# Six modulation rows as one evenly paced stream, from the first mixer to the second feed-forward

## Chip, cores and metric

The kernel runs on one core of a Trainium2 chip. The metric is the device time of one execution in microseconds (us). It is a single program of some 22,000 instructions that runs once per call, and everything in it is float32 (the matmuls use split pairs, below).

## The reference, cut to what matters

Two transformer blocks run one after the other on 256 tokens of width 1024. The first is feed-forward, mixer, feed-forward. The second is modulated by a condition vector `c`, and its context by `c_ctx`:

```python
x = first_block(x, ...)                    # ffn1, mixer1, ffn2
mod  = split(silu(c)     @ w_mod + b_mod, 6)     # six rows of 1024
modc = split(silu(c_ctx) @ w_mod + b_mod, 6)
h  = rmsnorm(x, norm1_g)  * (1 + mod[1])  + mod[0]
hc = rmsnorm(ctx, norm1_g) * (1 + modc[1]) + modc[0]
...                                        # second mixer on h, with states from hc
x  = x + mod[2] * mixer_out
h2 = rmsnorm(x, norm2_g) * (1 + mod[4]) + mod[3]
x  = x + mod[5] * conv_ffn(h2)
```

The change concerns the rows `mod[0..5]` of `c` and `modc[0..1]` of `c_ctx`: vectors that depend on no activations, only on the condition and the weights.

## The kernel before, in words

**Tiling.** Tokens are two blocks of 128 (`TB`). Each weight is streamed from HBM once, in pieces of 128x1024 floats (512 KB, queue of SP, L112, tile `raw`). A piece is split into a rounded high part on ACT (L127, `wh`) and a low part on DVE (L128, `wl`), and each product is three matmuls (`mm3`, L356 to L358). A ring of four split pieces and five raw pieces runs ahead of PE; DVE and ACT are thus needed for every piece that PE uses.

**Stages.** First feed-forward (`f1_gu`, 22 blocks of 48 matmuls, then `f1_dn`, 11 blocks of 24 wider ones), first mixer, its output projection `w_out_t`, second feed-forward (`f2_gu`, `f2_dn`), second mixer, third feed-forward. Behind each down or output projection `residual_norm` (L445) takes the four accumulators through ACT and DVE (sum of squares, gains, residual, norm) and PE transposes the result (L512). While that chain runs, PE has matmuls of the context: `ctx_attn` behind `f1_dn`, `ctx_mlstm` behind `w_out_t`, `ctx_ssd` (pieces `w_ctx` 8 to 10) behind `f2_dn`.

**Side work.** The order of all instructions is fixed when the program is written. `tick` (L197) advances a clock of nominal microseconds at each PE block, and generators registered by `side` (L212) take a step whenever their own time has come. A generator that yields a negative number asks for that much nominal time between steps. `join` (L225) steps a generator until it is done, at one place of the program, whatever its time.

**A modulation row.** `mod_rows` (L940) computes one row as sums of `silu(c)` times rows of `w_mod`, in two halves of 512 columns with eight steps each. A step issues one load of 128x512 floats (256 KB) from the ACT queue (L972), three steps ahead of its use, and one DVE instruction (L978 the first, L980 the others) into an accumulator. Behind eight steps the accumulator is split by ACT (L347) and DVE (L348), one step later PE adds it over the 128 partitions with a pair of matmuls on ones (L957, L958), and one step later DVE adds the bias (L961) and perhaps the gain (L963). Each row ends with three more steps without loads, in which the last sums are finished, and a store of the row by SP (L985). `mod_bcast` (L988) reads rows back where they are used.

**When.** The two rows of `c_ctx` run in the first feed-forward, 3.0 nominal us a step, and `ctx_norm` waits for them. Rows 0 and 1 of `c` start with the first mixer, 6.0 us a step. Rows 2 to 5 start when these and the states of `ctx_mlstm` are done, 2.0 us a step (`more`, L1726). Behind `f2_dn` L1750 joins that generator ahead of `residual_norm`.

Of the kernel before, what the change touches and what calls it, by code (L numbers as in the profile page):

```python
# [9 lines left out]
F32 = mybir.dt.float32  # L10
# [6 lines left out]
D = 1024  # L17
# [9 lines left out]
        ("s_norm_g", 4), ("s_d", 4), ("c", 8), ("c_ctx", 8))  # L27
NCOL = sum(w for _, w in COLS)
NU = 22
NV = 10  # L30
NW = 9
NRAW = 5
RING = 4
# [149 lines left out]
class Net:  # L183
# [753 lines left out]
            yield  # L937


    def mod_rows(self, j, c, gain, out, pace):  # L940


        nc, I = self.nc, self.I
        b = self.u([1, D])
        nc.sync.dma_start(b, I["b_mod_2"][:, j * D:(j + 1) * D])
        if gain is not None:
            g = self.u([1, D])
            nc.sync.dma_start(g, I[gain])
        steps = [(hf, k) for hf in range(2) for k in range(8)]
        ws, ahead, acc = [], 3, None  # L950

        def reduced(acc, hf):
            hi, lo = self.v([128, 512], F32R), self.v([128, 512], F32R)
            self.split(hi, lo, acc)
            yield
            p = self.psA([128, 512])
            nc.tensor.matmul(p[:1], self.onesr[:, :1], hi, start=True, stop=False)  # L957
            nc.tensor.matmul(p[:1], self.onesr[:, :1], lo, start=False, stop=True)  # L958
            yield
            x = self.halves(b)[hf]  # L960
            nc.vector.tensor_tensor(out=x, in0=p[:1], in1=x, op=OP.add)  # L961
            if gain is not None:
                nc.vector.scalar_tensor_tensor(x, x, 1.0, self.halves(g)[hf], op0=OP.add, op1=OP.mult)  # L963

        half = []
        for n in range(len(steps) + ahead + 3):
            for h in half:
                next(h, None)
            if n < len(steps):
                hf, k = steps[n]  # L970
                ws.append(self.v([128, 512]))
                nc.scalar.dma_start(ws[-1], I["w_mod"][j * 8 + k][:, hf * 512:hf * 512 + 512])  # L972
            if 0 <= n - ahead < len(steps):
                hf, k = steps[n - ahead]
                sc = self.silu[c][:, k:k + 1]
                if k == 0:
                    acc = self.v([128, 512])
                    nc.vector.tensor_scalar(acc, ws[n - ahead], sc, None, op0=OP.mult)  # L978
                else:
                    nc.vector.scalar_tensor_tensor(acc, ws[n - ahead], sc, acc, op0=OP.mult, op1=OP.add)  # L980
                if k == 7:
                    half.append(reduced(acc, hf))
            yield -pace
        row = self.dp.tile([1, D], F32, tag=f"mod{c}{j}", name=f"mod_{c}{j}")
        nc.sync.dma_start(row, b)  # L985
        out[c, j] = row

    def mod_bcast(self, c, j):  # L988
        t = self.u([128, D])
# [652 lines left out]
    def program(self, out):  # L1642
# [17 lines left out]
        self.weights.split()  # L1660
        back = self.spill(h, "res0")
        rope = self.side(self.rope_tables(), 40)
        self.mods = {}

        def setup():
            while not hasattr(self, "silu"):
                yield
            for j in range(2):
                yield from self.mod_rows(j, "c_ctx", (None, "norm1_g_2")[j], self.mods, 3.0)

        const = self.side(self.consts(), 4)
        prep = self.side(setup(), 6)
# [32 lines left out]
        self.join(rope, t)  # L1705
        back = self.spill(h, "res1")

        def rows(idx, pace):
            for j in idx:
                yield from self.mod_rows(j, "c", {1: "norm1_g_2", 4: "norm2_g_2"}.get(j), self.mods, pace)  # L1710

        prep = self.side(rows(range(2), 6.0))
        m = [self.u([128, 4, T]) for _ in range(2)]
        mT = self.mixer1(xT, m)
        self.xc = Split(self, 8)
# [7 lines left out]
        self.join(t)  # L1723
        back = self.spill(h, "res2")

        def more():  # L1726
            yield from self.until(states, prep0)
            yield from rows(range(2, 6), 2.0)

        prep0, prep = prep, self.side(more())  # L1730
        hT = self.ffn_up("f2_gu", xT, self.silu_mul)
        self.xc = Split(self, 8)
        cs = self.side(self.ctx_again())
# [1 line left out]
        def gains2(post, gain, shift):  # L1735
            gp["post"] = self.bcast(post) if isinstance(post, str) else self.mod_bcast("c", post)
            gp["pre"], gp["shift"] = self.mod_bcast("c", gain), self.mod_bcast("c", shift)
            gp["h"] = back()
            yield 8
            if isinstance(post, str):  # L1740
                nc.vector.tensor_scalar(gp["post"], gp["post"], 0.5, None, op0=OP.mult)
# [2 lines left out]

        def aside(i):
            if i == 3:
                gs.append(self.side(gains2("ffn2_post_g", 1, 0)))

        acc = self.down("f2_dn", NFF // 2, hT, aside)
        self.join(cs, prep, *gs)  # L1750
        xT, h = Split(self, 8), gp["h"]
        t = self.residual_norm(acc, h, gp["post"], True, gp["pre"], gp["shift"], xT)
        self.ctx_ssd(self.xc)
        self.join(t)
        back = self.spill(h, "res3")

        mT = self.mixer2(xT, lambda: gs.append(self.side(gains2(2, 4, 3))))
        acc = self.down("w_out_2", 4, mT, lambda i: self.weights.presplit(2 * i), 2)
        self.join(*gs)
        xT, h = Split(self, 8), gp["h"]  # L1760
        t = self.residual_norm(acc, h, gp["post"], False, gp["pre"], gp["shift"], xT, ((0, 0, 0, 1, 1, 1, 0, 1, 2, 3),))
        self.join(t)
        back = self.spill(h, "res4")
        hT = self.ffn_up("w_up_t", xT, self.conv_silu_mul)

        def last():
# [155 lines left out]
```

## Time and profile before

| what | value |
|---|---|
| time, median of 3 runs | 1292.15 us (1290.2 to 1292.22) |
| profiled execution: its time, its span | 1290.56 us, 1288.8 us |
| PE busy, DVE busy, ACT busy | 93%, 72%, 48% of the span |
| mean granted clock of TensorE | 0.971 of full speed |
| loads of `w_mod` | 128 of 256 KB, from the ACT queue |
| read from HBM | 241.46 MB, 194 GB/s over the span |

The span runs from the first to the last instruction; the time of an execution is 1.8 us longer here. The page gives busy shares of each engine and the same for 40 slices of the span. A PE that is busy 99% of a slice is the limit there, and whatever other engines do in that slice costs nothing as long as they keep up. A slice in which PE is idle is read from the timeline: the bracket at a row's end is the idle time of that engine just before the instruction and what released it. A clock of 1.00 is the higher of the two levels of TensorE, 2.4 GHz; 0.50 is the lower, 1.2 GHz.

### The profile page before, as it was taken

What the parts mean: (1) busy time and instruction counts of PE and PEld (TensorE: products, weight loads), DVE (VectorE), ACT (ScalarE), POOL (GpSimd) and SP (SyncE); (2) the same over time, 40 slices, a digit from 0 to 9 for tenths busy, and PEclk for the clock granted to TensorE, in tenths of its full rate; (3) what the DMA queues carried; (4) which work ended last, traced back from release to release, by engine and by line L of the source; (5) the groups of instructions that cost most, each with busy time, mean ns of one, the idle gap of its engine ahead of it and who ended that gap; (6) DMA issues with size and microseconds to landing.
All of it is one profiled execution on the core that took longest, in us unless ns stands there. A gap on an engine that the chain in (4) does not pass through costs nothing. (4 is left out here: it accounts for less than half of the span.)

```text
span 1288.8 us, 22199 instructions
## 1 busy us (share of the span) xinstructions
PE 1199.3 (93%) x8728; PEld 1115.0 (87%) x8728; DVE 934.0 (72%) x1603; ACT 624.1 (48%) x1063; POOL 66.9 (5%) x84
## 2 busy tenths in 40 slices
PE   7999998999999999999981699999999998999998
PEld 7999977999878889999860599999888897999977
DVE  4897857667766786767857878589666767888854
ACT  4454545455564464444420454556465344555542
POOL 0020000100000000000000001035100000000000
PEclk8999999999999999999995799999999998999999
DMA  7878785666343766657896355345413265555562
GB/s 265 273 229 256 257 291 195 206 218 218 123 135 116 292 199 221 222 188 247 299 338 216 100 195 190 133 156 172 143 54 100 98 209 216 172 173 181 179 241 85
DMA packets 80605, 251.32 MB, mean 195 GB/s; under 512 B 9523, under 2 KB 10851, under 8 KB 80502
## 3 DMA queue, kind: packets, MB, share of 16 engines
q1 hardware_dynamic: 61654, 215.85, 49.6%
q10 hardware_dynamic: 18432, 33.56, 7.8%
q0 software_dynamic: 416, 0.50, 0.4%
q8 instruction: 68, 1.11, 0.3%
q14 instruction: 35, 0.29, 0.1%
HBM read 241.46 MB, written 8.42 MB: 194 GB/s over the span
## 5 line engine op out<-in xcount | busy, mean ns | idle before, releaser
L128 DVE TENSOR_TENSOR wl<-raw,wh 128x1024 fp32r<-128x1024 f32 (+3 forms) x358 | 424.1, 1218 | 137.0 <-ACT wh L127 133.8
L356 PE MATMUL pB<-u,wh 128*128 128x256 f32 x1696 | 486.6, 287 | 0.7 <-ACT u L347 0.7
L358 PE MATMUL pB<-u,wl 128*128 128x256 f32 x1696 | 481.9, 284 | 1.0 <-DVE wl L128 1.0
L357 PE MATMUL pB<-u,wh 128*128 128x256 f32 x1696 | 481.5, 284 | 0.6 <-DVE u L348 0.3
L127 ACT ACTIVATE wh<-raw 128x1024 fp32r<-128x1024 f32 (+3 forms) x358 | 359.3, 1045 | 93.1 <-PE pB L358 33.8
L356 PEld LDWEIGHTS pB<-u,wh 128*128 128x128 f32 x1696 | 326.0, 192 | 9.4 <-issue 6.8
L358 PEld LDWEIGHTS pB<-u,wl 128*128 128x128 f32 x1696 | 326.0, 192 | 2.3 <-DVE wl L128 1.4
L357 PEld LDWEIGHTS pB<-u,wh 128*128 128x128 f32 x1696 | 326.0, 192 | 1.8 <-DVE u L348 1.4
L356 PE MATMUL pB<-wh,u 128*128 128x512 f32 (+3 forms) x614 | 208.1, 339 | 1.7 <-ACT wh L127 1.7
L357 PE MATMUL pB<-wl,u 128*128 128x512 f32 (+3 forms) x614 | 207.6, 338 | 2.2 <-DVE wl L128 2.0
L358 PE MATMUL pB<-wh,u 128*128 128x512 f32 (+3 forms) x614 | 206.5, 336 | 0.0
L357 PEld LDWEIGHTS pB<-wl,u 128*128 128x128 f32 x614 | 117.0, 191 | 15.7 <-DVE wl L128 5.0
L356 PEld LDWEIGHTS pB<-wh,u 128*128 128x128 f32 x614 | 117.0, 191 | 14.1 <-ACT wh L127 2.4
L358 PEld LDWEIGHTS pB<-wh,u 128*128 128x128 f32 x614 | 117.0, 190 | 11.7
L428 POOL TENSOR_TENSOR rs<-ms,nhalf 128x1 f32<-128x1 f32 (+2 forms) x30 | 28.4, 946 | 877.2 <-DVE ms L422 874.5
L520 ACT ACTIVATE w<-pB 128x256 f32<-128x256 f32 x44 | 16.9, 383 | 116.7 <-PE pB L358 116.3
L980 DVE SCALAR_TENSOR_TENSOR v<-v,silu_c,v 128x512 f32<-128x512 f32 x84 | 62.8, 748 | 12.3 <-DMA v<-w_mod 11.2
L1006 DVE SCALAR_TENSOR_TENSOR w<-pB,cols,w 128x255 f32<-128x255 f32 x120 | 49.6, 476 | 15.8 <-ACT w L1001 10.1
L521 DVE SCALAR_TENSOR_TENSOR w<-w,pB 128x256 f32<-128x256 f32 x44 | 18.5, 420 | 50.2 <-ACT w L520 49.8
L957 PE MATMUL pA<-v,onesr 128*1 128x512 f32 x16 | 7.3, 456 | 42.5 <-ACT v L347 42.5
L356 PE MATMUL pA<-wh,u 128*128 128x256 f32 x132 | 38.5, 292 | 2.4 <-ACT u L347 1.7
L957 PEld LDWEIGHTS pA<-v,onesr 128*1 128x1 f32 x16 | 1.3, 83 | 45.2 <-ACT v L347 45.0
(365 smaller groups left out, 1421.9 us busy)
## 6 DMA issues: line engine op xcount, KB each, us to landing
raw<-f_gu SPq DMA_DIRECT2D x88, 512.0 KB
v<-w_mod ACTq DMA_DIRECT2D x128, 256.0 KB
raw<-w_lat SPq DMA_DIRECT2D x64, 512.0 KB
raw<-f_dn SPq DMA_DIRECT2D x44, 512.0 KB
raw<-w_up_t SPq DMA_DIRECT2D x44, 512.0 KB
raw<-w_ctx SPq DMA_DIRECT2D x22, 512.0 KB
raw<-w_down_t SPq DMA_DIRECT2D x22, 512.0 KB
raw<-w_in_g SPq DMA_DIRECT2D x16, 512.0 KB
```

The source lines that it names most:

```text
L127: nc.scalar.activation(hi, r, AF.Copy)
L128: nc.vector.tensor_tensor(out=lo, in0=r, in1=hi.bitcast(F32), op=OP.subtract)
L356: nc.tensor.matmul(out, a[0], b[0], start=first, stop=False)
L357: nc.tensor.matmul(out, a[0], b[1], start=False, stop=False)
L358: nc.tensor.matmul(out, a[1], b[0], start=False, stop=last)
L428: self.nc.gpsimd.tensor_tensor(out=r, in0=ms, in1=self.nhalf[:, :width], op=OP.pow)
L520: nc.scalar.activation(th, p[:, 0], AF.Tanh, scale=0.5)
L521: nc.vector.scalar_tensor_tensor(th, th, 1.0, p[:, 0], op0=OP.add, op1=OP.mult)
L957: nc.tensor.matmul(p[:1], self.onesr[:, :1], hi, start=True, stop=False)
L980: nc.vector.scalar_tensor_tensor(acc, ws[n - ahead], sc, acc, op0=OP.mult, op1=OP.add)
L1006: nc.vector.scalar_tensor_tensor(y[j][:, o], p[:, j, x], tap(t, i), y[j][:, o], op0=OP.mult, op1=OP.add)
```

## The change

One call of `mod_rows` now takes a list of rows and runs their steps on end: the loads of a row's first steps are issued while the last sums of the row before are finished. The bias and the gain are loaded by halves, into the tiles `v` (12 buffers instead of 10) and no longer into the larger tiles `u`, and each half is added and stored by itself. All six rows of `c` are one generator that starts with the first mixer, 4.2 nominal us a step, and 2.6 from the second feed-forward on; the order of rows is 0, 1, 2, 4, 3, 5. The join of the rows behind `f2_dn` is gone: `need_rows` steps the generator before the place where rows are read back, if they are not done by then, and a join stands behind the second mixer.

```diff
-NV = 10
+NV = 12
...
-    def mod_rows(self, j, c, gain, out, pace):
+    def mod_rows(self, rows, pace):
         nc, I = self.nc, self.I
-        b = self.u([1, D])
-        nc.sync.dma_start(b, I["b_mod_2"][:, j * D:(j + 1) * D])
...
-        steps = [(hf, k) for hf in range(2) for k in range(8)]
+        steps = [(r, hf, k) for r in rows for hf in range(2) for k in range(8)]
...
+            x = self.v([1, 512])
+            nc.sync.dma_start(x, I["b_mod_2"][:, j * D + hf * 512:j * D + hf * 512 + 512])
...
+            nc.sync.dma_start(self.rows[c, j][:, hf * 512:hf * 512 + 512], x)
+            if hf == 1:
+                self.mods[c, j] = self.rows[c, j]
...
-            yield -pace
-        row = self.dp.tile([1, D], F32, tag=f"mod{c}{j}", name=f"mod_{c}{j}")
-        nc.sync.dma_start(row, b)
-        out[c, j] = row
+            yield -pace[0]
+
+    def need_rows(self, side, *keys):
+        while not all(k in self.mods for k in keys):
+            side.step()
...
-            for j in range(2):
-                yield from self.mod_rows(j, "c_ctx", (None, "norm1_g_2")[j], self.mods, 3.0)
+            yield from self.mod_rows([("c_ctx", 0, None), ("c_ctx", 1, "norm1_g_2")], [3.0])
...
-        def rows(idx, pace):
-            for j in idx:
-                yield from self.mod_rows(j, "c", {1: "norm1_g_2", 4: "norm2_g_2"}.get(j), self.mods, pace)
-
-        prep = self.side(rows(range(2), 6.0))
+        pace = [4.2]
+        gain = {1: "norm1_g_2", 4: "norm2_g_2"}
+        rows = self.side(self.mod_rows([("c", j, gain.get(j)) for j in (0, 1, 2, 4, 3, 5)], pace))
...
-        def more():
-            yield from self.until(states, prep0)
-            yield from rows(range(2, 6), 2.0)
-
-        prep0, prep = prep, self.side(more())
+        pace[0] = 2.6
...
             if i == 3:
+                self.need_rows(rows, ("c", 0), ("c", 1))
                 gs.append(self.side(gains2("ffn2_post_g", 1, 0)))
...
-        self.join(cs, prep, *gs)
+        self.join(cs, *gs)
...
-        mT = self.mixer2(xT, lambda: gs.append(self.side(gains2(2, 4, 3))))
+        def aside():
+            self.need_rows(rows, ("c", 2), ("c", 4), ("c", 3))
+            gs.append(self.side(gains2(2, 4, 3)))
+
+        mT = self.mixer2(xT, aside)
...
         back = self.spill(h, "res4")
+        self.join(rows)
```

What this does to the order of instructions is shown at three places. Names ending in `wh` or `wl` are split weights, `pB` the accumulators of a projection, `pA` a smaller one.

PE, between the last matmul of `f2_dn` and the first ones of `w_ctx` 8, before (one more pair stands ahead of these rows, behind that last matmul):

```order
L957 MATMUL pA_7754<-v_7750,onesr 1x512
L958 MATMUL pA_7754<-v_7751,onesr 1x512
L957 MATMUL pA_7803<-v_7795,onesr 1x512
L958 MATMUL pA_7803<-v_7796,onesr 1x512
L957 MATMUL pA_7827<-v_7823,onesr 1x512
L958 MATMUL pA_7827<-v_7824,onesr 1x512
L957 MATMUL pA_7875<-v_7867,onesr 1x512
L958 MATMUL pA_7875<-v_7868,onesr 1x512
L957 MATMUL pA_7898<-v_7894,onesr 1x512
L958 MATMUL pA_7898<-v_7895,onesr 1x512
L356 MATMUL pA_7941<-u_7221,wh_7719 128x256
L357 MATMUL pA_7941<-u_7222,wh_7719 128x256
```

and in the changed kernel at the same place:

```order
L356 MATMUL pB_7440<-wh_7872,u_5676 128x512
L357 MATMUL pB_7440<-wl_7873,u_5676 128x512
L358 MATMUL pB_7440<-wh_7872,u_5677 128x512
L356 MATMUL pB_7440<-wh_7878,u_5676 128x512
L357 MATMUL pB_7440<-wl_7879,u_5676 128x512
L358 MATMUL pB_7440<-wh_7878,u_5677 128x512
L356 MATMUL pA_7971<-u_7433,wh_7922 128x256
L357 MATMUL pA_7971<-u_7434,wh_7922 128x256
L358 MATMUL pA_7971<-u_7433,wl_7923 128x256
```

Six pairs (L957, L958) stood between the last matmul of `f2_dn` and `w_ctx`; none does now. The last pair of the stream stands 48 matmuls earlier, inside `f2_dn`. On DVE the last step of the stream stands in front of the last six splits of weights ahead of the residual chain.

DVE, in the middle of `f2_gu`, before (`w` and `u` are the activation function of a block; L521, L523 and L351 stand once in each block):

```order
L521 SCALAR_TENSOR_TENSOR w_6017<-w_6017,pB_5921 128x256
L523 TENSOR_TENSOR w_6020<-w_6017,pB_5921 128x256
L128 TENSOR_TENSOR wl_6023<-raw_5801,wh_6022 128x1024
L128 TENSOR_TENSOR wl_6029<-raw_5878,wh_6028 128x1024
L351 SCALAR_TENSOR_TENSOR u_5580<-w_6020,u_5579 128x256
L980 SCALAR_TENSOR_TENSOR v_5411<-v_5803,silu_c,v_5411 128x512
```

and in the changed kernel (L984 is L980 of before):

```order
L521 SCALAR_TENSOR_TENSOR w_6137<-w_6137,pB_6038 128x256
L523 TENSOR_TENSOR w_6140<-w_6137,pB_6038 128x256
L128 TENSOR_TENSOR wl_6143<-raw_5899,wh_6142 128x1024
L128 TENSOR_TENSOR wl_6149<-raw_5989,wh_6148 128x1024
L984 SCALAR_TENSOR_TENSOR v_5909<-v_6035,silu_c,v_5909 128x512
L351 SCALAR_TENSOR_TENSOR u_5669<-w_6140,u_5668 128x256
L984 SCALAR_TENSOR_TENSOR v_5909<-v_6080,silu_c,v_5909 128x512
```

A block of `f2_gu` carries two steps instead of one, and so does each block of `f2_dn` up to the tenth.

DVE, in the residual chain behind `w_out_t`, before (the chain of the second token block, then L478, which the first transposes wait for):

```order
L128 TENSOR_TENSOR wl_5273<-raw_5143,wh_5272 128x1024
L438 TENSOR_TENSOR ssq_5283<-ssq_5283,ssq_5280 128x1
L457 TENSOR_TENSOR u_5210<-pB_5039,u_5063 128x512
L457 TENSOR_TENSOR u_5210<-pB_5040,u_5063 128x512
L422 TENSOR_SCALAR ms_988_5289<-ssq_5283 128x1
L460 SCALAR_TENSOR_TENSOR u_5068<-u_5210,rs_989_5291,u_5068 128x512 x2
L478 SCALAR_TENSOR_TENSOR u_5209<-u_5067,rs_973_5235,u_5065 128x512 x2
```

and in the changed kernel:

```order
L128 TENSOR_TENSOR wl_5344<-raw_5213,wh_5343 128x1024
L984 SCALAR_TENSOR_TENSOR v_4931<-v_5155,silu_c,v_4931 128x512
L438 TENSOR_TENSOR ssq_5355<-ssq_5355,ssq_5352 128x1
L457 TENSOR_TENSOR u_5281<-pB_5111,u_5135 128x512
L457 TENSOR_TENSOR u_5281<-pB_5112,u_5135 128x512
L422 TENSOR_SCALAR ms_1013_5361<-ssq_5355 128x1
L460 SCALAR_TENSOR_TENSOR u_5140<-u_5281,rs_1014_5363,u_5140 128x512 x2
L348 TENSOR_TENSOR v_5392<-v_4931,v_5391 128x512
L982 TENSOR_SCALAR v_5401<-v_5194,silu_c 128x512
L478 SCALAR_TENSOR_TENSOR u_5280<-u_5139,rs_998_5306,u_5137 128x512 x2
```

Three instructions of the rows have moved in ahead of L478 there, and one more (L984) stands ahead of the L478 of the second token block. In the first feed-forward the rows of `c_ctx` end some eight weight pieces earlier, and `ctx_norm` with its transposes (L1154) ends inside `f1_dn`; before, its last transposes stood behind it.

## Rows read from the trace of the kernel before

**Rows 1.** Page, parts 1 and 2: PE busy; 40 slices of 32.2 us, in tenths.

```profile
PE 1199.3 (93%) x8728; PEld 1115.0 (87%) x8728; DVE 934.0 (72%) x1603; ACT 624.1 (48%) x1063; POOL 66.9 (5%) x84
...
PE   7999998999999999999981699999999998999998
...
PEclk8999999999999999999995799999999998999999
```

**Rows 2.** Waits of PE, 560 to 800 us: waiter, releaser: us in total, times, longest.

```profile
PE pA L957 <- ACT v L347: 42.5, 5, 9.9
```

**Rows 3.** Timeline of PE around the stall: start us, us, line, operation, [idle before].

```profile
670.94 0.39 PE L358 MATMUL pB<-wh,u 128*128 128x512 f32 x1
...
681.24 0.59 PE L957 MATMUL pA<-v,onesr 128*1 128x512 f32 x1 [9.45 <-ACT v L347]
...
720.61 0.41 PE L356 MATMUL pA<-u,wh 128*128 128x256 f32 x1
...
733.80 1.32 PE L512 MATMUL pB<-ident,u 128*128 128x128 f32 x8 [2.23 <-DVE u L480]
```

**Rows 4.** Windows around it: us; busy PE, PEld, DVE, ACT, POOL; clock; DMA; GB/s.

```profile
675.00:685.00 10.00, 1.18 (x2) 0.16 (x2) 5.62 (x8) 0.63 (x1) 0.00 (x0) 0.50 0.56 180
...
735.00:745.00 10.00, 8.83 (x72) 8.19 (x71) 10.00 (x20) 7.38 (x14) 0.97 (x3) 1.00 0.31 107
```

**Rows 5.** Timelines of DVE and then ACT in the stall.

```profile
692.08 0.69 DVE L348 TENSOR_TENSOR v<-v,v 128x512 fp32r<-128x512 f32 x1 [0.69 <-ACT v L347]
692.69 0.48 DVE L978 TENSOR_SCALAR v<-v,silu_c 128x512 f32<-128x512 f32 x1
...
719.36 0.58 ACT L436 ACTIVATE v<-pB 128x512 f32<-128x512 f32 x1
```

**Rows 6.** Page, a step; windows, steps on DVE; timeline of PE, a covered pair.

```profile
L980 DVE SCALAR_TENSOR_TENSOR v<-v,silu_c,v 128x512 f32<-128x512 f32 x84 | 62.8, 748 | 12.3 <-DMA v<-w_mod 11.2
...
672.00:721.00 49.00, 27.41 (x38) 0.52 0.64 212
...
619.08 0.40 PE L957 MATMUL pA<-v,onesr 128*1 128x512 f32 x1
...
619.55 0.39 PE L356 MATMUL pB<-wh,u 128*128 128x512 f32 x1
```

**Rows 7.** Windows of both feed-forwards: columns as in rows 4.

```profile
40.00:60.00 20.00, 20.00 (x169) 20.00 (x168) 15.49 (x24) 9.28 (x15) 0.00 (x0) 1.00 0.87 298
60.00:80.00 20.00, 20.00 (x167) 19.77 (x167) 19.21 (x40) 9.43 (x15) 4.56 (x8) 1.00 0.80 257
520.00:540.00 20.00, 20.00 (x167) 19.77 (x166) 14.33 (x22) 8.94 (x14) 0.00 (x0) 1.00 0.68 221
620.00:640.00 20.00, 20.00 (x89) 16.32 (x88) 17.40 (x19) 9.97 (x11) 0.00 (x0) 1.00 0.84 294
640.00:660.00 20.00, 19.06 (x83) 15.24 (x82) 9.63 (x11) 5.68 (x6) 0.00 (x0) 1.00 0.92 324
```

**Rows 8.** Timelines of PE and then ACT at the end of the first feed-forward.

```profile
208.94 0.40 PE L358 MATMUL pB<-wh,u 128*128 128x512 f32 x1
209.17 1.04 PE L1154 MATMUL pA<-ident,u 128*128 128x128 f32 x8
211.89 0.38 PE L356 MATMUL pA<-wh,u 128*128 128x256 f32 x1 [1.68 <-ACT u L347]
...
224.80 1.32 PE L512 MATMUL pB<-ident,u 128*128 128x128 f32 x8 [1.51 <-DVE u L478]
...
212.67 0.59 ACT L436 ACTIVATE v<-pB 128x512 f32<-128x512 f32 x1
```

**Rows 9.** Timeline of PE behind the first mixer's output projection; waits in its heads.

```profile
459.72 1.32 PE L512 MATMUL pB<-ident,u 128*128 128x128 f32 x8 [1.13 <-DVE u L478]
...
466.63 1.04 PE L512 MATMUL pB<-ident,u 128*128 128x128 f32 x8
...
PE pB L730 <- DVE v L723: 4.2, 3, 1.5
```

More of the change, by code (lines that the diff above doesn't have):

```diff
@@ L937, in heads_T, with reduced @@
             yield
-    def mod_rows(self, j, c, gain, out, pace):
+    def mod_rows(self, rows, pace):
         nc, I = self.nc, self.I
-        b = self.u([1, D])
-        nc.sync.dma_start(b, I["b_mod_2"][:, j * D:(j + 1) * D])
-        if gain is not None:
-            g = self.u([1, D])
-            nc.sync.dma_start(g, I[gain])
-        steps = [(hf, k) for hf in range(2) for k in range(8)]
+        steps = [(r, hf, k) for r in rows for hf in range(2) for k in range(8)]
         ws, ahead, acc = [], 3, None
-        def reduced(acc, hf):
+        def reduced(acc, c, j, gain, hf):
             hi, lo = self.v([128, 512], F32R), self.v([128, 512], F32R)
             self.split(hi, lo, acc)
+            x = self.v([1, 512])
+            nc.sync.dma_start(x, I["b_mod_2"][:, j * D + hf * 512:j * D + hf * 512 + 512])
+            if gain is not None:
+                g = self.v([1, 512])
+                nc.sync.dma_start(g, I[gain][:, hf * 512:hf * 512 + 512])
             yield
@@ L959, in reduced @@
             yield
-            x = self.halves(b)[hf]
             nc.vector.tensor_tensor(out=x, in0=p[:1], in1=x, op=OP.add)
             if gain is not None:
-                nc.vector.scalar_tensor_tensor(x, x, 1.0, self.halves(g)[hf], op0=OP.add, op1=OP.mult)
+                nc.vector.scalar_tensor_tensor(x, x, 1.0, g, op0=OP.add, op1=OP.mult)
+            if hf == 0:
+                self.rows[c, j] = self.dp.tile([1, D], F32, tag=f"mod{c}{j}", name=f"mod_{c}{j}")
+            nc.sync.dma_start(self.rows[c, j][:, hf * 512:hf * 512 + 512], x)
+            if hf == 1:
+                self.mods[c, j] = self.rows[c, j]
         half = []
@@ L969, in mod_rows @@
             if n < len(steps):
-                hf, k = steps[n]
+                (c, j, gain), hf, k = steps[n]
                 ws.append(self.v([128, 512]))
@@ L973, in mod_rows @@
             if 0 <= n - ahead < len(steps):
-                hf, k = steps[n - ahead]
+                (c, j, gain), hf, k = steps[n - ahead]
                 sc = self.silu[c][:, k:k + 1]
@@ L981, in mod_rows @@
                 if k == 7:
-                    half.append(reduced(acc, hf))
-            yield -pace
-        row = self.dp.tile([1, D], F32, tag=f"mod{c}{j}", name=f"mod_{c}{j}")
-        nc.sync.dma_start(row, b)
-        out[c, j] = row
+                    half.append(reduced(acc, c, j, gain, hf))
+            yield -pace[0]
+    def need_rows(self, side, *keys):
+        while not all(k in self.mods for k in keys):
+            side.step()
     def mod_bcast(self, c, j):
@@ L1662, in program @@
         rope = self.side(self.rope_tables(), 40)
-        self.mods = {}
+        self.mods, self.rows = {}, {}
         def setup():
```

## The prediction, made before the run

> **What bounds the kernel now.** I read the page first. PE is busy 93% of the span, and of its 40 slices nearly all stand at 8 or 9 tenths; one stands at 1 and its neighbour at 6 [rows 1]. In these two slices the clock falls to its lower level as well. So PE is the limit nearly everywhere, extra work of DVE, ACT and the queues is free as long as they keep up with it, and one stretch of some 50 us is limited by something else. The view of waits names it: PE waits 42.5 us in five pieces of up to 9.9 us for ACT's L347, and it is L957 that waits, the sum over partitions of a modulation row [rows 2]. The timeline shows the place: the last matmul of the second feed-forward starts at 670.94, the next matmul that any activation needs at 720.61, and between them stand only the pairs L957, L958, each behind some nine us of idle [rows 3]. The windows show what runs meanwhile: DVE at 56%, PE at 1.18 us of 10, clock 0.50 [rows 4]. Of the 96 steps of the six rows, 38 lie there, 27.41 us of DVE, and DVE also waits for loads [rows 6]. They stand in one lump because the generator of rows 2 to 5 starts late and is then joined ahead of the residual chain.
>
> The residual chain itself (sum of squares to transposes) is a second limit behind each projection: PE waits for DVE at L512 [rows 3, 8, 9]. In the feed-forwards PE is at 20.00 of 20 us in all windows shown but one [rows 7].
>
> **The change part by part.** The sum is made against the profiled execution, 1290.56 us.
>
> *The lump goes: -48.5 us.* From the last matmul at 670.94 to the first transposes at 733.80 pass 62.9 us [rows 3]. In the changed order nothing of the rows is left between them. What is late next is the residual chain: before, from the first sum of squares at 719.36 [rows 5] to 733.80 it took 14.4 us, and in the changed kernel it can start with the last matmul. PE has 96 matmuls of `w_ctx` to do meanwhile, 0.12 us each (167 in 20 us [rows 7]), 11.5 us, so it still waits some 2 us for the chain as it does now. 62.9 - 14.4 = 48.5. The ends: 51.4, if PE's own 11.5 us were all; 47.0, if the stretch took 15.9 us, as the one behind the first feed-forward does (208.94 to 224.80 [rows 8]). I take the chain's, since it is the same chain with the same instructions.
>
> *Pairs that were free cost PE time: +2.8 us.* Six pairs move from the lump into stretches where PE is full. A covered pair takes 0.47 us (619.08 to 619.55 [rows 6]). The ends are 2.8 and, if each also waits for its split by ACT and DVE, more; the covered pair shows no wait, so I take 2.8.
>
> *The moved steps themselves: 0.* 38 steps of 0.748 us [rows 6], with their loads on ACT's queue, their splits and sums, now lie beside matmuls. In `f2_gu` a block gets two steps instead of one. A block lasts 48 x 0.12 = 5.8 us, so 20 us hold 3.5 blocks: DVE goes from 14.33 us [rows 7] by 3.5 x 0.75 = 2.6 and by some 0.6 for splits and sums (an estimate from one L348 of 0.69 and one bias of the same size per eight steps) to 17.5 of 20. In the first feed-forward DVE was at 19.21 of 20 with the same kind of work, rows of `c_ctx` included, and PE still at 20.00 [rows 7]. That is the nearest row, and I take 0. What is queued behind a step on DVE is the low part of the next weights (L128); the ring of four pieces covers a delay of that size. The other end comes from the only row where DVE is full: 10.00 of 10, with PE at 8.83 [rows 4], a loss of 12%.
>
> The loads add 3.5 x 262 KB in 20 us, 46 GB/s, to the 221 of `f2_gu`, 267 in all; the first feed-forward ran at 257 and 298 with PE full [rows 7]. In `f2_dn` steps get rarer (two a block; before, two or three), from 294 GB/s down. The small loads and stores of halves on SP's queue double in number, 2 KB each; a store waits for DVE's sum, and behind it stand the weight loads, which wait for DVE's splits of the same place anyway: 0.
> The Trainium skill, "DMA: Bandwidth & Descriptors", section "Issuing engines are not separate DMA queues", says that transfers from any queue end on the same 16 engines and interleave, so by it ACT's queue gives the loads no room of their own; the trace bears it out only so far as PE lost 0.94 us in the fullest window, 324 GB/s [rows 7]. By the rule the moved loads delay weights wherever the engines are full; that is the third rival below, and it changes nothing in the sum here.
>
> *The first mixer: +1.0 us.* At 4.2 instead of 6.0 some ten steps more fall between its start and the projection, 7.5 us of DVE. They are hidden where matmuls of weights run. In the heads PE waits for DVE's softmax, now 4.2 us in three places [rows 9]; a step in front of such a DVE instruction lengthens it. Ends: 0 and 7.5; nearer to 0, since PE waits in so few places.
>
> *The chain behind `w_out_t`: +2.7 us.* A step (0.75), a split (0.69) and a first step (0.48) [rows 5, 6] now stand on DVE ahead of L478, for which the transposes at 459.72 already wait 1.13 us [rows 9], and one more step (0.75) ahead of the second L478, whose transposes start at 466.63 with no slack to speak of. 0.75 + 0.69 + 0.48 + 0.75 = 2.67. Ends: 0, if the second is absorbed and DVE takes the others while it waits for POOL; 5, if the idle also brings the lower clock for a few us, as it did behind the first feed-forward.
>
> *The first feed-forward's end: -3.1 us.* Before, `ctx_norm` was late: its eight transposes (1.04 us) stood behind the last matmul, ACT had to evacuate and split them before the sum of squares could start at 212.67, PE waited 1.68 for the same, and the transposes of the chain came at 224.80 [rows 8]. In the changed order all of that lies eight pieces earlier. Then the sum of squares starts at some 207 to 208 and the chain (212.67 to 224.80, 12.1 us) ends by 220, before PE's 11.5 us of matmuls. PE is the limit: 15.9 - 0.2 - 11.5 = 4.1 us less, of which the transposes, still done inside `f1_dn`, take back 1.04. Ends: -4.1 and 0.
>
> *The sum.* 1290.56 - 48.5 + 2.8 + 0 + 1.0 + 2.7 - 3.1 = 1245.5. The median of the runs is 1.6 us above the profiled execution, so 1247 for the median, 3.5% less than 1292.15. All ends of the terms together give 1239 to 1260 without the rivals; they are not to be expected at once.
>
> **The rivals.**
> *DVE becomes the limit in the second feed-forward.* For it: 17.5 of 20 us is an average, and a split and a sum come in lumps. Against it: the first feed-forward at 19.21. If half of its 33 blocks (186 us) lost the 12% of the full window, that is 11 us: 1258.
>
> *The DMA engines become the limit there.* For it: 324 GB/s and a PE that lost 0.94 of 20 us [rows 7]. If all 186 us lost as much, 8.7 us: 1256. Against it: 267 is expected, and 298 was harmless.
>
> *Slower than before: the loads block ACT.* ACT issues each load of `w_mod` in its own order, between the high parts of weights (L127). If the buffer or the completion that a load must wait for is late, ACT stands, then L128, then PE. It costs the whole gain of 46 us once each of the 96 loads holds PE up for 0.48 us; if each waited for one DVE step, 0.75, that is 72 us: 1319. Against it: 32 loads of `c_ctx` in the first feed-forward, at a similar rate, left PE at 20.00 [rows 7].
>
> *The change does not do what it says*: the stream is late and the rest is stepped at one place again. The order speaks against it, the last step stands inside `f2_dn`; 1290 if it were so.
>
> *More than forecast.* The loss of 0.94 us in `f2_dn` goes, the mixer's terms are hidden, and two more buffers free waits in the second mixer: 1240.
>
> **How the numbers follow.** Forecast 0.74; DVE 0.10; DMA 0.06; more 0.06; slower 0.03; no effect 0.01. The likeliest gives 1247, its own range by the terms 1241 to 1254. The range given, 1240 to 1258, reaches to three of the rivals and leaves out the slow one, the one without effect and part of the DVE case. A measurement of this kernel tells 0.2%, 2.6 us, from no change. Faster by more: 0.74 + 0.10 + 0.06 + 0.06 = 0.96; within: 0.01; slower: 0.03.
>
> **What would show it right or wrong.** The two low slices gone, the clock at 1.00 throughout the second feed-forward and behind it; no wait of L957 above a us; 14 to 15 us from the last matmul of `f2_dn` to L512, with an idle of some 2 us; DVE at 0.85 to 0.9 in `f2_gu` with PE at 20.00 of 20; PE's idle ahead of L512 behind `w_out_t` grown from 1.1 to some 3 us, and none behind `f1_dn`. The prediction is wrong if PE waits for L127 or L128 in the second feed-forward, or if another wait of tens of us stands where rows are read back.

## The result, and the profile after

The changed kernel takes 1244.38 us (median of 4 runs, 1243.18 to 1246.42) against 1292.18 for the kernel before: a ratio of 0.9635, with a 95% interval of 0.9618 to 0.9652, so 3.65% less. The profiled execution took 1244.19, its span is 1242.4. In a later set of runs the same kernel took 1242.59, so a difference of 2 us between sets says nothing.

Page, parts 1 and 2, of the changed kernel, the rows that answer to [rows 1]:

```profile
PE 1195.7 (96%) x8728; PEld 1116.3 (90%) x8728; DVE 929.4 (75%) x1603; ACT 623.1 (50%) x1063; POOL 67.8 (5%) x84
...
PE   7999999899998979999999999999899998999998
...
PEclk8999999999999999999999999999999998999999
```

The two low slices are gone, and the clock no longer falls in the middle of the program. PE's busy time and DVE's are what they were; only the span is shorter. The waits of PE between 560 and 800 us, as in [rows 2] (waiter, releaser: us in total, times, longest):

```profile
PE pB L512 <- DVE u L480: 2.5, 2, 1.8
PE pA L1095 <- DVE nd L1389: 1.0, 1, 1.0
```

The 42.5 us of L957 are gone and nothing of that size stands in their place. The timeline of PE, as in [rows 3], and under it ACT's, at the end of the second feed-forward:

```profile
676.26 0.39 PE L358 MATMUL pB<-wh,u 128*128 128x512 f32 x1
676.48 0.28 PE L356 MATMUL pA<-u,wh 128*128 128x256 f32 x1
...
687.04 1.32 PE L512 MATMUL pB<-ident,u 128*128 128x128 f32 x8 [1.77 <-DVE u L480]
...
672.60 0.60 ACT L436 ACTIVATE v<-pB 128x512 f32<-128x512 f32 x1 [0.30 <-PE pB L358]
```

From the last matmul of `f2_dn` to L512 it is 10.8 us where it was 62.9. Two windows of the second feed-forward, columns as in [rows 4]:

```profile
520.00:540.00 20.00, 20.00 (x168) 19.77 (x167) 16.95 (x27) 9.40 (x15) 0.00 (x0) 1.00 0.84 268
...
640.00:660.00 20.00, 20.00 (x90) 16.32 (x89) 13.04 (x16) 6.70 (x7) 0.00 (x0) 1.00 1.00 377
```

DVE took the added steps (16.95 of 20 us, before 14.33 [rows 7]) with PE still at 20.00.

To see where the time went, the matmuls of weights (L356 to L358) are counted in both timelines, in which they come in the same order, and the start of the same one is compared. Start of a matmul in us, before and after:

```
place                                         before    after   after - before   this stage
first matmul                                   16.45    16.66        +0.21
last matmul of f1_dn                          208.94   208.91        -0.03          -0.2
behind the chain of the first feed-forward    229.31   227.12        -2.19          -2.2
w_out_t begins to run                         447.07   446.94        -0.13          +2.1  (first mixer)
behind w_out_t's chain                        482.81   488.18        +5.37          +5.5
last matmul of f2_dn                          670.94   676.26        +5.32          -0.1  (second feed-forward)
behind the lump and the chain                 737.35   690.60       -46.75         -52.1
late in the program                          1282.25  1235.60       -46.65          +0.1
```

### The profile page after: what moved, and what is told of

Same layout as the page of the kernel before. It is cut to its first block, busy times and chain, and to the rows that moved or that the text cites. A ratio compares the mean times of both kernels' runs of the same rounds, so it can differ in the third digit from the quotient of the medians.

```text
span 1242.4 us, 22210 instructions
## 1 busy us (share of the span) xinstructions
PE 1195.7 (96%) x8728; PEld 1116.3 (90%) x8728; DVE 929.4 (75%) x1603; ACT 623.1 (50%) x1063; POOL 67.8 (5%) x84
## 5 line engine op out<-in xcount | busy, mean ns | idle before, releaser
L128 DVE TENSOR_TENSOR wl<-raw,wh 128x1024 fp32r<-128x1024 f32 (+3 forms) x358 | 423.8, 1218 | 143.2 <-ACT wh L127 140.3
L356 PE MATMUL pB<-u,wh 128*128 128x256 f32 x1696 | 486.0, 287 | 0.7 <-ACT u L347 0.7
L358 PE MATMUL pB<-u,wl 128*128 128x256 f32 x1696 | 481.3, 284 | 1.0 <-DVE wl L128 1.0
L127 ACT ACTIVATE wh<-raw 128x1024 fp32r<-128x1024 f32 (+3 forms) x358 | 358.8, 1045 | 94.0 <-PE pB L358 29.4
L356 PEld LDWEIGHTS pB<-u,wh 128*128 128x128 f32 x1696 | 325.4, 192 | 9.7 <-issue 7.0
L358 PEld LDWEIGHTS pB<-u,wl 128*128 128x128 f32 x1696 | 325.2, 192 | 2.3 <-DVE wl L128 1.4
L356 PE MATMUL pB<-wh,u 128*128 128x512 f32 (+3 forms) x614 | 208.0, 339 | 2.9 <-ACT wh L127 1.6
L358 PE MATMUL pB<-wh,u 128*128 128x512 f32 (+3 forms) x614 | 206.2, 336 | 0.0
L356 PEld LDWEIGHTS pB<-wh,u 128*128 128x128 f32 x614 | 116.9, 190 | 15.3 <-ACT wh L127 1.8
L358 PEld LDWEIGHTS pB<-wh,u 128*128 128x128 f32 x614 | 116.9, 190 | 11.9
L520 ACT ACTIVATE w<-pB 128x256 f32<-128x256 f32 x44 | 16.9, 384 | 113.5 <-PE pB L358 113.1
L984 DVE SCALAR_TENSOR_TENSOR v<-v,silu_c,v 128x512 f32<-128x512 f32 x84 | 62.5, 744 | 0.3
L521 DVE SCALAR_TENSOR_TENSOR w<-w,pB 128x256 f32<-128x256 f32 x44 | 18.4, 419 | 29.5 <-ACT w L520 29.5
L357 PE MATMUL pA<-wl,u 128*128 128x256 f32 x132 | 38.7, 293 | 1.8 <-DVE wl L128 1.8
L356 PE MATMUL pA<-wh,u 128*128 128x256 f32 x132 | 39.0, 296 | 0.7 <-ACT wh L127 0.7
L358 PE MATMUL pA<-wh,u 128*128 128x256 f32 x132 | 38.4, 291 | 0.0
```

The source lines that it names most:

```text
L127: nc.scalar.activation(hi, r, AF.Copy)
L128: nc.vector.tensor_tensor(out=lo, in0=r, in1=hi.bitcast(F32), op=OP.subtract)
L356: nc.tensor.matmul(out, a[0], b[0], start=first, stop=False)
L357: nc.tensor.matmul(out, a[0], b[1], start=False, stop=False)
L358: nc.tensor.matmul(out, a[1], b[0], start=False, stop=last)
L520: nc.scalar.activation(th, p[:, 0], AF.Tanh, scale=0.5)
```

## The experiments

Changes of place within a kernel are told by the same comparison of matmul starts, here against the changed kernel. Each edit is to the changed kernel, where nothing else is said.

**The lump moved, but not spread.** An edit of the kernel before:

```
-        self.join(cs, prep, *gs)          # behind f2_dn
+        self.join(cs, *gs)
         ...
         back = self.spill(h, "res4")
+        self.join(prep)
```

> The kernel before, with one edit: the generator of rows 2 to 5 is no longer joined ahead of the residual chain behind the second feed-forward, but behind the next chain (res4). Its generator stays in two parts with its breaks between rows and its old paces (6.0, 2.0); the steps left over run on into the second mixer. Theory (the uncovered lump at the join is the whole of the cost, and how the rows are spread matters little): about 52 us go, as in the changed kernel, two to eight pairs are covered, and the w_out chain and the first feed-forward stay as before: 1292 - 52 + 3 = 1243, range 1238 to 1250. Rival (the stream without breaks and its even spread are needed, since steps that spill into the residual chain and the second mixer cost what they cost in the lump): the some 40 steps left at the join cost 0.75 us each behind it, so 30 us of the gain are lost: 1265 to 1275.

It took 1273.9 us, ratio 0.9882 (0.9857 to 0.9906) to the kernel before: the theory fell and the rival held. At the last matmul of `f2_dn` PE was 5.5 us ahead of the changed kernel and behind the chain, at 703 us, 2.5 late; so far the theory was near. But at the end of the second mixer's first part, at 860 us, it was 29.7 us late. Timelines of PE, then DVE, then POOL there:

```profile
848.13 0.59 PE L957 MATMUL pA<-v,onesr 128*1 128x512 f32 x1 [3.69 <-ACT v L347]
852.58 0.59 PE L958 MATMUL pA<-v,onesr 128*1 128x512 f32 x1 [3.86 <-DVE v L348]
...
845.87 1.22 DVE L980 SCALAR_TENSOR_TENSOR v<-v,silu_c,v 128x512 f32<-128x512 f32 x1
847.01 1.64 DVE L1006 SCALAR_TENSOR_TENSOR w<-pB,cols,w 128x255 f32<-128x255 f32 x4
848.58 3.35 DVE L128 TENSOR_TENSOR wl<-raw,wh 128x1024 fp32r<-128x1024 f32 x2
851.85 0.68 DVE L348 TENSOR_TENSOR v<-v,v 128x512 fp32r<-128x512 f32 x1
...
844.81 3.56 POOL L1129 TENSOR_TENSOR w<-u,rot 128x256 f32<-128x256 f32 x4 [2.55 <-DVE u L1120]
849.13 1.71 POOL L1131 TENSOR_TENSOR u<-w,w 128x256 f32<-128x256 f32 x1
```

DVE has work of its own there that PE waits for, so the 32 steps between 703 and 860 us cost 27 us again, 0.85 each. Taking the lump away from its place is worth 16.5 us here, about a third of the gain; the rest needs the steps to go where DVE is free.

**A smaller lump put back.**

```
-        pace[0] = 2.6
+        pace[0] = 4.0
         ...
-        self.join(cs, *gs)                # behind f2_dn
+        self.join(cs, rows, *gs)
```

> The changed kernel, with the stream slowed in the second feed-forward (4.0 instead of 2.6) and joined again ahead of the residual chain: 18 of 96 steps (15 loads) are then left for that place, where before it were 38. Theory (what costs is the uncovered lump, 52 us for 38 steps, 1.4 us each, mostly by steps): 18 x 1.3 to 1.4 = 23 to 25 us more than the changed kernel, 1268 to 1270, PE waiting at L957 for ACT L347 in two or three pieces again. Rival (the gain comes from the stream without breaks and the two more buffers, so that even the steps left over run fast): 18 x 0.75 = 13 us or less, 1257 or below.

1260.81 us, 0.9779 (0.9757 to 0.9801): between the two. PE loses 19.0 us from the end of `f2_dn` to behind the chain, 18 steps at 1.05 us. So the lump is the cause of the cost, but a step in it was cheaper than the 52.1 us / 38 = 1.37 of before. The timeline of DVE in the lump, of this kernel, then of the kernel before, and DVE's waits in the latter from 671 to 720 us:

```profile
685.06 4.66 DVE L984 SCALAR_TENSOR_TENSOR v<-v,silu_c,v 128x512 f32<-128x512 f32 x6
690.48 0.69 DVE L348 TENSOR_TENSOR v<-v,v 128x512 fp32r<-128x512 f32 x1 [0.76 <-ACT v L347]
```

```profile
685.16 0.75 DVE L980 SCALAR_TENSOR_TENSOR v<-v,silu_c,v 128x512 f32<-128x512 f32 x1 [1.37 <-DMA v<-w_mod]
686.70 4.69 DVE L980 SCALAR_TENSOR_TENSOR v<-v,silu_c,v 128x512 f32<-128x512 f32 x6 [0.79 <-DMA v<-w_mod]
```

```profile
DVE v L980 <- DMA v<-w_mod: 7.6, 8, 2.1
```

Behind a break between rows the kernel before waits for loads that it could not issue earlier, 7.6 us in the lump in all; the stream has them ready. Over 38 steps that is 0.20 of the 0.32 us by which a step was dearer; what makes the rest is not shown, and no run put the breaks back into the lump.

**The same with 10 buffers** (`NV = 10`), to tell the buffers from the stream:

> The kernel with the lump back (18 steps joined ahead of the residual chain), with 10 instead of 12 buffers for the loaded rows. There a step cost 1.03 us, in the kernel before 1.39. Theory (more loads in flight made the steps of the lump quicker): with 10 buffers DVE waits for loads again and a step costs 1.3 to 1.4, 1266 to 1268. Rival (it is the breaks between rows that made a step dear before, as each row drained and filled the queue of loads): no difference, 1260 to 1262.

1262.95 us, 0.979 (0.9763 to 0.9818), PE losing 19.6 us at the lump against 19.0. The time lies 1.0 us above the rival's range and 3 below the theory's: the buffers are not the reason.

**10 buffers in the changed kernel** (`NV = 10`):

> The changed kernel with 10 instead of 12 buffers, which is this part of the change undone alone. Theory (steps that lie beside matmuls come so far apart that two buffers more do nothing): 1243 to 1246. Rival (a load that waits for its buffer holds up the weights' high parts on ACT): PE waits for L127 in the second feed-forward, 1248 or more.

1246.19 us, 0.9652 (0.9629 to 0.9676). PE never waits for L127 in the second feed-forward; it stands 2.1 us behind at the end, and 2.4 of delay come in one place in the first mixer, behind 360 us, where the clock was 0.85 for 10 us and 1.00 in the changed kernel. The same dip comes and goes in other kernels (below). The dearer end of the theory's range was missed by 0.2; the two buffers do nothing that these runs can tell.

**The stream broken up again, spread evenly.**

```
+        def one_by_one():
+            for j in (0, 1, 2, 4, 3, 5):
+                yield from self.mod_rows([("c", j, gain.get(j))], pace)
+        rows = self.side(one_by_one())
...
-        pace = [4.2]                      # and 2.6 in the second feed-forward
+        pace = [3.05]                     # and 1.9
```

> The changed kernel with the stream broken up again: each of the six rows drains before the next begins to load, as in the kernel before, and only the places are spread evenly (paces 3.05 and 1.9, so that the last step stays inside the second feed-forward). Theory (the gain comes from where the steps lie, not from the stream without breaks, which matters only where steps are uncovered): within 4 us of the changed kernel, the difference being pairs that meet their splits late where steps now stand three to a block, 1244 to 1249. Rival (a row's break costs some 2.5 us wherever it is, as it did in the lump): five breaks, 12 us, 1256 or more.

1246.56 us, 0.9665 (0.9635 to 0.9695), 4.0 above the changed kernel of its set. The theory held: in the second feed-forward it loses 1.1 us against the changed kernel; another 3.0 are lost in the first mixer, where the clock was lower for a while (0.83 and 0.70 in two stretches), and 1.8 behind 860 us. So nearly all of the gain is the even spread over places where DVE has room; that the stream has no breaks showed, if at all, only for steps that nothing covers. The halves of the bias and the new order of the rows were not tried by themselves.

**ctx_norm as late as before.**

```
...
-  ... ("c_ctx", 1, "norm1_g_2")], [3.0])
+  ... ("c_ctx", 1, "norm1_g_2")], [3.47])
```

> The changed kernel, with the two rows of c_ctx in the first feed-forward at a pace of 3.47 instead of 3.0, so that ctx_norm falls behind the last matmul as it did before. Theory (taking ctx_norm forward is what gains 3 us there): 2 to 4 us slower than the changed kernel, 1246.5 to 1248.5, with the transposes L512 behind f1_dn back at some 15 us behind the last matmul. Rival (the gain there is from something else, such as where the loads of w_ctx fall): within 1 us, 1243.5 to 1245.5.

1246.26 us, 0.9662 (0.9646 to 0.9679). From the first matmul to behind the chain PE loses 2.5 us, 2.2 of them from the last matmul of `f1_dn` on, as the theory said; 1.9 us more come in the first mixer, with the clock at 0.70 in 388 to 392. The time by itself, 1.9 above the changed kernel's in another set, lies between the two ranges and does not tell.

**A pause over the chain behind `w_out_t`.**

```
         xT, h = Split(self, 8), gp["h"]   # behind w_out_t
+        rows.ready += 14.0
...
-        pace[0] = 2.6
+        pace[0] = 2.4
```

> The changed kernel, with the stream paused over the residual chain behind w_out (14 us added to its due time there) and a pace of 2.4 instead of 2.6 in the second feed-forward so that it ends at the same place. Theory (the 6.5 us that the changed kernel loses around that chain come from the step, split, first step and second step on DVE ahead of L478, and from the pair): 4 us less, 1240, range 1239 to 1241.5, with the transposes L512 waiting about 1.1 us again and the clock staying up. Rival (the loss comes from the order in w_out itself, the wait for L915 and the pairs there, not from the chain): within 1 us of the changed kernel, 1243.5 to 1245.

1247.41 us, 0.9678 (0.9652 to 0.9703): no gain. Yet around the chain the pause gave 3.0 us, less than the 4 expected: the idle ahead of L512 fell from 3.91 to 2.26 and not to 1.1. More was lost in the second feed-forward, 6 us, most of it at three pairs; another 3 came in the first mixer, where the clock was lower for a while (0.83 and 0.68 in two stretches). Timelines of PE at the chain and at the dearest pair, and of DVE there:

```profile
462.59 1.32 PE L512 MATMUL pB<-ident,u 128*128 128x128 f32 x8 [2.26 <-DVE u L478]
...
621.28 0.39 PE L957 MATMUL pA<-v,onesr 128*1 128x512 f32 x1 [1.50 <-ACT v L347]
622.81 0.39 PE L958 MATMUL pA<-v,onesr 128*1 128x512 f32 x1 [1.15 <-DVE v L348]
...
619.79 2.36 DVE L128 TENSOR_TENSOR wl<-raw,wh 128x1024 fp32r<-128x1024 f32 x2 [0.53 <-ACT wh L127]
622.07 0.69 DVE L348 TENSOR_TENSOR v<-v,v 128x512 fp32r<-128x512 f32 x1
```

The split of the row's sum stands behind two low parts of weights on DVE, and PE reaches the pair that needs it first.

**The same, with the pair one step later in the second feed-forward.**

```
             yield                         # split -> pair
+            if pace[0] < 2.5:
+                yield
...
-        for n in range(len(steps) + ahead + 3):
+        for n in range(len(steps) + ahead + 4):
```

> The kernel with the pause behind w_out and the pace of 2.4, with one edit: in the second feed-forward a pair (L957, L958) is issued one step later behind its split than before. Theory (the pause gains 3 us at the chain, and what it lost in the second feed-forward was pairs that PE reached ahead of their splits, 1.50 + 1.15 us at one and less at others, not a DVE that is full): no wait of L957 or L958 above half a us in the second feed-forward, PE at 19.9 of 20 there, time 1241 to 1242.5. Rival (at 2.4 DVE itself is too full there): PE still loses 5 us, 1246 to 1248.

1242.07 us, 0.9617 (0.959 to 0.9644). The theory held: no wait for a split is left there, PE is at 179.2 of 180 us between 480 and 660, and the pairs there stand 12 or 24 matmuls later. The rival, a full DVE, is out at this pace. Whether the kernel is quicker than the changed one this run cannot tell: its times run from 1236.83 to 1244.36, and the changed kernel was not run beside it.

**Every step's DVE work twice.**

```
+                if c == "c":
+                    nc.vector.scalar_tensor_tensor(ws[n - ahead], ws[n - ahead], sc, ws[n - ahead], op0=OP.mult, op1=OP.add)
```

> The changed kernel with a second DVE instruction of the same size (0.75 us) behind each of the 84 accumulating steps of the six rows; it writes into the loaded tile, which nothing reads any more. Theory (the steps are free only because DVE has some 3 us in 20 left in the second feed-forward): there are about 60 steps there, 45 us of DVE more over nine windows of 20 us with 16.9 busy, so 21.8 for 20: PE loses some 9% of 180 us, 16 us, and the chain behind w_out 1.5 more, 1258 to 1270. Rival (what DVE does beside the matmuls does not matter, since PE is fed by the ring of pieces): within 3 us, 1244 to 1247.5.

1273.26 us, 0.9862 (0.9837 to 0.9888), 3.3 above the theory's range. The second feed-forward lost 19.2 us, where 16 were forecast, and the stretch around `w_out_t` 2.5; another 7.4 came in the first mixer, which the expectation had left out. Two windows of the second feed-forward, columns as in [rows 4], and PE's waits from 485 to 700 us:

```profile
520.00:540.00 20.00, 20.00 (x166) 19.53 (x165) 19.69 (x30) 10.05 (x16) 0.00 (x0) 1.00 0.80 254
560.00:580.00 20.00, 17.62 (x144) 16.96 (x144) 19.65 (x30) 8.73 (x13) 0.00 (x0) 1.00 0.73 238
...
PE pA L958 <- DVE v L348: 9.4, 5, 2.6
```

So the added work did cost PE time, as the theory said. But DVE was as full in the first window, where PE lost nothing, as in the second, and about half of the loss stands at pairs that waited for their splits. That a DVE without room is the cause, and not splits that come late in its order, this run does not show.

**Every step's load twice.**

```
+                if c == "c":
+                    nc.scalar.dma_start(self.v([128, 512]), I["w_mod"][j * 8 + k][:, 512 - hf * 512:1024 - hf * 512])
```

> The changed kernel with a second load of 256 KB for each of the 96 steps of the six rows, on ACT's queue, into a tile that nothing reads. Theory (neither the DMA engines nor ACT's issue of loads are a limit there; the second feed-forward ran at 377 GB/s with PE at 20.00 of 20): 46 GB/s more in the first part of the second feed-forward costs nothing, in its second part up to 3 us, 1244 to 1249. Rival (loads hold up ACT or the weights): PE waits for L127 or L128 there, 8 us or more, 1253 to 1265.

1254.64 us, 0.9725 (0.9696 to 0.9754), 12.0 above the changed kernel of its set. The time fell into the rival's range. The stretch around `w_out_t` lost 1.8 us, `f2_gu` 1.8 and `f2_dn` 7.9. Two windows of the last; ACT's waits from 600 to 690 us; and what SP's queue (q1) and ACT's (q10) moved from 610 to 670 us, packets, MB and share of the engines, in the changed kernel and then in this one:

```profile
620.00:640.00 20.00, 18.51 (x81) 14.48 (x80) 13.95 (x18) 7.92 (x10) 0.00 (x0) 1.00 1.00 374
640.00:660.00 20.00, 18.86 (x82) 14.81 (x81) 14.66 (x17) 7.50 (x8) 0.00 (x0) 1.00 1.02 378
...
ACT wh L127 <- DMA raw<-f_dn: 11.9, 5, 5.1
ACT wh L127 <- DMA v<-w_mod: 11.4, 2, 6.2
```

```profile
q1 hardware_dynamic: 4155, 15.10, 69.2%
q10 hardware_dynamic: 2160, 3.93, 19.6%
```

```profile
q1 hardware_dynamic: 3500, 12.73, 56.2%
q10 hardware_dynamic: 5262, 9.58, 44.0%
```

In a window the engines move no more than the 377 GB/s of the changed kernel's fullest, and fewer of the bytes are weights; now PE waits, so the changed kernel stands near the edge there. But ACT also stands longer for loads of `w_mod`, 11.4 us where it was 5.0 in the changed kernel, and the second loads take turns in the same 12 buffers. Full engines and loads that hold up ACT, the rival's two halves, are not told apart by this run. PE's own waits from 600 to 690 us, 2.9 us for weights (L127, L128) and 3.6 at pairs, fit both.

**The pause from the start of `w_out_t`** (the pause and the later pair, 14 us more of pause ahead of `w_out_t`, pace 2.2), beside **the changed kernel again**:

> The kernel with the pause and the later pair, with the pause 14 us longer, from the start of the w_out projection to the end of the chain behind it, and a pace of 2.2 instead of 2.4 so that the stream still ends inside the second feed-forward. Theory (the 2.2 us that the changed kernel lost within w_out itself come from a pair and steps that now lie elsewhere): 1 to 2 us less than with the pause alone, 1240 to 1241.5. Rival (DVE is too full in the second feed-forward at 2.2 even with the later pair, up to 3 steps to a block): what is gained is lost again there, 1242.5 to 1246.

> The changed kernel itself, unaltered, beside the others of this set on one chip, so that differences of 2 or 3 us can be told. Every theory: 1243 to 1246.5.

1240.38 us (1238.65 to 1242.09), ratio 0.9618 (0.9592 to 0.9644), against 1242.59 (1241.73 to 1242.88), ratio 0.9632 (0.9607 to 0.9656): 2.2 us less, 0.2%, with ranges that overlap. The first time lies in its theory's range, the second 0.4 below the expected one. Its windows of the second feed-forward hold PE at 20.00 in all nine, so the rival is out; the fullest of DVE:

```profile
500.00:520.00 20.00, 20.00 (x168) 19.77 (x167) 19.06 (x30) 10.73 (x17) 0.00 (x0) 1.00 0.84 277
```

and the transposes behind `w_out_t` wait as little as before the change [rows 9]:

```profile
461.33 1.32 PE L512 MATMUL pB<-ident,u 128*128 128x128 f32 x8 [0.76 <-DVE u L478]
```

The wait of L915 (below) stayed. This is the quickest of the kernels run, by a margin at the limit of what these runs tell.

## Why the prediction was right, point by point

The forecast of 1247 was 2.6 us above the result. Its mechanism held: the lump goes, nothing of its size takes its place, and the moved steps are free in the second feed-forward. Its terms were less good than their sum: the lump and the moved steps came out 5.5 us better than forecast, the two chains and the first mixer 3.6 us worse. That the sum came so near is in part luck.

**The lump** was forecast at -48.5, with ends -51.4 and -47.0; it is -52.1, beyond both. The chain itself was sized rightly: from the first sum of squares at 672.60 to L512 at 687.04 it takes 14.4 us, as before. The step that failed is "it can start with the last matmul". It starts 3.7 us ahead of it, since the first half of the first token block's sums is complete 18 matmuls before the last. And PE has 72 matmuls ahead of L512, not 96 (676.48 to 685.27, then the 1.77 of idle), so the end that took PE as the limit was wrong as well.

**The pairs and the moved steps**: +2.8 and 0 were forecast, -0.1 is measured over the second feed-forward. Of the six moved pairs four stand there (8 against 4), one in the first mixer and one behind `w_out_t`; each costs 0.46 us, 2.8 in all, as forecast. In the second feed-forward PE got back what its four cost: at 640 to 660 it had 19.06 of 20 us [rows 7] and now 20.00, a gain that the prediction named only under "more than forecast". The load was taken as said, but the 0 is less safe than the first feed-forward's 19.21 made it look: DVE was at 16.9 on average, 19.06 was harmless with the later pair, and with the work doubled PE lost 2.4 of 20 in one window with DVE at 19.65 and nothing in another at 19.69. What is lost first is not DVE's time but the order: with the pause and two tenths less pace, pairs met their splits late.

**The first mixer**: +1.0 with ends 0 and 7.5; measured +2.1, 0.5 of it one of the pairs. 1.3 is one place, where a step stands on DVE ahead of what PE needs next. PE's wait between 420 and 475 us, then DVE's timeline:

```profile
PE pB L356 <- DVE v L915: 1.3, 1, 1.3
```

```profile
426.77 0.75 DVE L984 SCALAR_TENSOR_TENSOR v<-v,silu_c,v 128x512 f32<-128x512 f32 x1
427.44 0.68 DVE L915 SCALAR_TENSOR_TENSOR v<-u,pB 128x512 f32<-128x512 f32 x1
```

In the heads the wait of L730 grew from 4.2 [rows 9] to 4.8. Nearer to 0 than to 7.5, as chosen.

**The chain behind `w_out_t`**: +2.7 with ends 0 and 5; measured +5.5. Without the pair there (468.14, 0.5 us, which the prediction counts among its six) it is 5.0, the upper end and near twice the value taken. The instructions named are there, and the idle ahead of L512 grew by 2.8, from 1.13 [rows 9] to 3.91. What the value left out is the lower clock, which stood only in the upper end. Timeline of PE, and windows of the changed kernel and then of the kernel before:

```profile
461.93 1.97 PE L512 MATMUL pB<-ident,u 128*128 128x128 f32 x8 [3.91 <-DVE u L478]
```

```profile
460.00:464.00 4.00, 2.07 (x10) 2.08 (x11) 3.97 (x9) 3.95 (x10) 1.06 (x1) 0.56 0.18 69
464.00:468.00 4.00, 4.00 (x23) 4.00 (x23) 4.00 (x6) 0.53 (x1) 0.38 (x1) 0.59 0.62 223
```

```profile
460.00:464.00 4.00, 3.99 (x35) 3.75 (x34) 3.21 (x6) 3.28 (x7) 0.55 (x1) 1.00 0.30 89
464.00:468.00 4.00, 4.00 (x37) 4.00 (x36) 4.00 (x7) 3.24 (x6) 0.00 (x0) 1.00 0.79 242
```

The pause, which takes the rows' instructions away from there, brings 3.0 us back; the longer pause brings 5.4 us back from the start of `w_out_t` to behind its chain.

**The first feed-forward's end**: -3.1 forecast; -2.2 from the last matmul of `f1_dn` to behind the chain and -0.2 ahead of it, -2.4 in all. The size was near, by another way. PE was to be the limit, with no idle ahead of L512; but here too it has 72 matmuls of `w_ctx` and not the 96 of the sum. The timelines of ACT and then PE show the chain as the limit:

```profile
208.36 1.06 ACT L127 ACTIVATE wh<-raw 128x1024 fp32r<-128x1024 f32 x1 [3.93 <-DMA raw<-w_ctx]
209.32 0.58 ACT L436 ACTIVATE v<-pB 128x512 f32<-128x512 f32 x1
...
221.27 1.77 PE L512 MATMUL pB<-ident,u 128*128 128x128 f32 x8 [3.35 <-DVE u L478]
```

ACT stands 3.93 us for a load of weights that is ahead of the sum of squares in its order, so the chain starts at 209.32 and not at 207 or 208, and its 11.95 us stay the limit. Up to L512 3.5 us are gained (15.9 behind the last matmul before, 12.4 now); behind it, with the clock at 0.69 from 220 to 224 us, 1.3 of them are lost again. That ctx_norm's place is what gains was borne out by the kernel that put it back (2.5 us).

**The rivals.** That DVE becomes the limit is out for the changed kernel; twice the DVE work brought a loss, about half of it at pairs. That the DMA engines become the limit (the second rival in the prediction's list, which it once calls the third) is out too, but by little: the doubled loads cost 7.9 us in `f2_dn`, near the 8.7 that the rival was priced at for the whole feed-forward, though loads that hold up ACT may have a part in it. The Trainium skill, "DMA: Bandwidth & Descriptors", section "Issuing engines are not separate DMA queues", has loads of all queues interleave on the same engines. The doubled loads agree: with the engines full, SP's queue moved 12.73 MB of weights in 60 us instead of 15.10 while ACT's moved 9.58 instead of 3.93. That loads block ACT: ACT did stand for a `w_mod` load in the changed kernel, once for 5.0 us between 600 and 680, without PE waiting for it.

## What to carry to other kernels

Work that is off the critical path has to be placed, not only moved: it is free where its engine has room and where nothing that the limiting engine needs next is queued behind it, and the same steps cost 0.85 to 1.4 us each elsewhere. Spread it evenly over the stretch with the most room, pause it over the short chains that the limiting engine waits for, and keep a consumer on that engine a good step behind its producer. When forecasting such a gain, find where the next chain starts in the trace, and not where the last matmul ends.

## What the runs showed of the hardware

- A step takes 0.75 us, but 1.22 where POOL runs tensor operations at the same time (845.87, POOL from 844.81 for 3.56 us), and two low parts took 3.35 us instead of 2.36 (848.58, POOL until 850.84). The Trainium skill, "SBUF — State Buffer", section "SBUF: two separate sides", says that a DVE operation with two inputs in SBUF and a GpSimd operation that reads SBUF exclude each other for the length of an instruction. The rows agree that they collide; DVE's are lengthened by some 0.5 us each. At another place of the same kernel, DVE and then POOL, the one that began first was not lengthened: a step that began 0.2 us ahead of a POOL operation took 0.74, and that operation 1.12, where the shortest like it there took 0.73.

```profile
835.04 0.74 DVE L980 SCALAR_TENSOR_TENSOR v<-v,silu_c,v 128x512 f32<-128x512 f32 x1
...
835.26 1.12 POOL L1129 TENSOR_TENSOR w<-u,rot 128x256 f32<-128x256 f32 x1 [2.64 <-ACT u L350]
```

- The clock of the first mixer differs from run to run with the same instructions in the same order: 1.00 and 0.68 in these rows of the changed kernel and of the kernel with the pause, whose first edit comes later in the program. Such dips cost some 2 us, and make single traces differ by as much.

```profile
384.00:388.00 4.00, 4.00 (x32) 2.79 (x30) 2.93 (x12) 1.92 (x3) 0.00 (x0) 1.00 0.27 111
```

```profile
384.00:388.00 4.00, 4.00 (x21) 2.89 (x22) 2.24 (x9) 2.07 (x3) 0.00 (x0) 0.68 0.50 192
```

- 377 GB/s with the engines' share at 1.00 left PE at 20.00 of 20 us in one window, and 374 to 378 GB/s with more asked left it at 18.5 and 18.9: the rate alone doesn't tell whether it is enough, though ACT was held up as well there.
